# A two-layer retention and attention trunk: first sweep over three token tiles by weight slab, a later turn of the last residual tile, and a tail prepared in the last head

## The chip, the cores and the metric

The kernel runs on one core of one Trainium2 chip. Its engines run side by side: TensorE (PE in the profile, its weight loads PEld), VectorE (DVE), ScalarE (ACT), GpSimd (POOL) and SyncE (SP), which issues DMAs. The metric is the device time of one execution in microseconds (us). Lower is better.

## The reference

Two layers over 1024 tokens of width 1024, all in 32-bit floats. Layer 0 is gated retention with 8 heads (query and key 128 wide, values 256), layer 1 is gated differential attention with 8 heads. Cut to what matters:

```python
h = rmsnorm(x, pre_norm[0]); proj = h @ w_in_a          # q, k, v, gate
o = retention(rope(q), rope(k), v)                      # chunkwise, state carried on, group norm
x = x + rmsnorm((o * silu(gate)) @ w_out_a, post_norm[0])
kv = rmsnorm(x, kv_norm) @ w_kv                         # keys (two per head, rotary), values
h = rmsnorm(x, pre_norm[1]); q, gate = split(h @ w_in_b)
w = softmax(q1 k1) - lam * softmax(q2 k2)               # masked by blocks
o = rmsnorm(w @ v, sub_norm) * (1 - lambda_init)
x = x + rmsnorm((o * silu(gate)) @ w_out_b, post_norm[1])
```

## The kernel before

Tokens are cut into 8 tiles (`c`, `t` or `b`) of 128, the model width into 8 slabs (`s` or `f`) of 128. Every operand of a large product is held as a pair of numbers of a shorter 32-bit form: `split` (L85 on) copies the value into the high part on ACT (L87, or L90 with a gain) and takes the rest into the low part on DVE (L88, L91). `mm3` (L100) multiplies such pairs with three matmuls, high by high, high by low, low by high.

**Retention.** `load_x` brings one tile's transposed x from DRAM and splits it into `xT`; `stats_x` brings the same tile untransposed, sums its squares (L131) and makes scales (L134 to L136) that multiply v and the outputs; `load_qkv` and `load_gate` bring a head's weights. The 64 units (head `h` outside, tile `c` inside) then run in a software pipeline: in unit i, `gemm_qkv` forms q, k and v of tile c in one 512-wide PSUM tile (24 matmuls); `score` of the unit before (L234, mask L235, split L236 and L237) sits in the middle; `rotate` applies the rotary embedding (L207 and L208 on DVE, sum L209 on POOL) and splits v; `combine` of the unit before forms values, carries the state and normalises; `gate_and_transpose` forms the gate (24 matmuls of 256) and transposes q and k (L218, L219), followed on ACT by a copy, Silu (L221) and splits. The first two units share one sweep (`early`): for each slab, tile 0 and then tile 1.

**First output projection.** It runs in two groups of heads. The last step of a tile makes the residual tile `y` (L373). `fin1(t)` gives two functions that transpose half of it each (`quarter`, L284) and split it into `x2T`. Sixteen `gate_unit`s follow, two halves of the gate's columns times 8 tiles. `woven` says which slab of which gate unit is followed by a turn: the turn of tile 6 lies in unit 0 after slabs 2 and 5, and the turn of tile 7 in unit 1 after slabs 3 and 6.

**Attention.** 64 units again; each forms q, k and v of one head and tile (`gemm_piece`, 24 matmuls of 384), rotates (`rotate_b`, L527 and L528 on DVE, L529 on POOL), and in the next unit transposes (`transpose_b`, L538). `attend` yields, two units behind, the pieces for one block of queries: `scores` (L552; fill and maximum L558 and L559, exponent L560, difference of the two softmaxes L565), `turn` (transposes L577) and `values` (L588, copy L591, norm, and a store to the DRAM buffer `og2d`).

**Tail.** `load_wob` brings and splits the second output projection's weights during head 7. `out_prep(t)` loads `og` and the gate `g` of a tile from DRAM, multiplies them (L626), transposes (L632) and splits. `out_gemm(t)` is a generator of 16 steps of three matmuls, with square and sum (L651), product with the post gain (L652), the norm (L653, L105 and L106, the power on POOL) and the residual (L657) after them. What remains of `attend` is interleaved with its steps.

The program is written as one stream; each engine executes its own instructions in the order that the framework's scheduler gave them, so an instruction that waits holds up those behind it on its engine. All DMAs of before are issued by SP, in order. Staging buffers (`st_`) come from one pool of four. PSUM has two slots each of three kinds, g, s2 (1024 wide) and s.

## Time and profile before

| | us |
|---|---|
| median of 3 runs (lowest, highest) | 1515.81 (1514.84, 1515.99) |
| the profiled execution | 1515.86 |
| its span | 1513.9 |
| PE busy | 1480.3 (98%) |
| DVE busy | 784.6 (52%) |
| ACT busy | 629.5 (42%) |
| POOL busy | 268.9 (18%) |

A row of a timeline gives the start, the duration, the engine, the program's line, the operation, output and inputs with their shapes, how often it stands there in a row, and in brackets the idle time of the engine ahead of it with what ended it. `SPq L658` is a DMA issued by SP, `PEq` the sequencer of PE. Time outside the span (1515.86 less 1513.9, about 2 us) is the launch. An engine's busy share says nothing on which wait ends last; that is read stage by stage, below.

### The profile page before, as it was taken

The numbers are of one execution on the slowest core, as the hardware profiler recorded it, in microseconds if no ns is written. First come the engines' busy times: TensorE is split into PE (matmuls) and PEld (weight loads), VectorE is DVE, ScalarE is ACT, GpSimd is POOL, SyncE is SP. The second block draws the span as 40 slices with busy tenths as digits, with TensorE's granted clock in tenths as the row PEclk, the third lists the DMA queues.
The fourth block names the chain that finished last, engine by engine and source line by source line (L and its number), as shares of the span: only waits on it lengthen the run. The fifth ranks groups of instructions, "written<-read, shape, count | busy, mean of one in ns | idle before, by whom it ended". The sixth has DMA issues, their size and how long they took to land.

```text
span 1513.9 us, 23779 instructions
## 1 busy us (share of the span) xinstructions
PE 1480.3 (98%) x8752; PEld 1297.4 (86%) x8752; DVE 784.6 (52%) x1976; ACT 629.5 (42%) x1607; POOL 268.9 (18%) x470
## 2 busy tenths in 40 slices
PE   6999999999999999999999999999999999998998
PEld 5888998888989888888888788988988988987886
DVE  4764645454545544541155502667567567577443
ACT  5542423242423332332244513556556455555421
POOL 0322221222222222200000000222222222222100
PEclk9999999999999999999999999999999999999999
DMA  7430302021111211252345522011011011023352
GB/s 262 158 111 15 95 18 88 22 77 36 59 53 46 63 54 66 70 184 98 140 167 174 174 70 83 30 32 52 22 41 51 12 52 51 11 93 120 113 173 84
DMA packets 70308, 125.63 MB, mean 83 GB/s; under 512 B 7600, under 2 KB 40752, under 8 KB 70192
## 3 DMA queue, kind: packets, MB, share of 16 engines
q1 hardware_dynamic: 70192, 124.11, 25.1%
q8 instruction: 69, 1.13, 0.3%
q14 instruction: 47, 0.39, 0.1%
HBM read 94.72 MB, written 29.36 MB: 82 GB/s over the span
## 4 chain that ended last, share of the span: by engine, by line
PE 85%; DVE 5%; ACT 3%; DMA 3%; issue 3%; POOL 1%; SPq 0%; DVEq 0%; POOLq 0%; ACTq 0%
PE pg L100 57%; PE ps L100 15%; PE ps L552 3%; PE ps L588 3%; PE ps L577 2%; PE ps L284 1%; ACT pr L560 1%; PE ps L234 1%; DVE wbh L91 1%; DMA stw<-in_wa 1%; DMA xr<-in_x 1%; DMA stg<-in_wa 1%; PE ps L538 1%; PE ps L632 1%; DVE m L559 0%
## 5 line engine op out<-in xcount | busy, mean ns | idle before, releaser
L100 PE MATMUL pg<-wq,xT 128*128 128x512 f32 x1536 | 387.0, 402 | 9.9 <-ACT wq L90 7.2
L100 PEld LDWEIGHTS pg<-wq,xT 128*128 128x128 f32 x1536 | 281.2, 190 | 65.9 <-ACT wq L90 7.2
L100 PE MATMUL pg<-wbh,x2T 128*128 128x384 f32 x1536 | 334.4, 353 | 0.0
L100 PEld LDWEIGHTS pg<-wbh,x2T 128*128 128x128 f32 x1536 | 256.3, 189 | 13.0 <-issue 9.2
L106 POOL TENSOR_TENSOR m<-m,mhalf 128x1 f32<-128x1 f32 x152 | 83.8, 551 | 648.2 <-DVE m L105 556.5
L100 PE MATMUL ps<-wg,xT 128*128 128x256 f32 x1536 | 195.4, 283 | 0.4 <-DVE wg L91 0.4
L100 PEld LDWEIGHTS ps<-wg,xT 128*128 128x128 f32 x1536 | 189.3, 192 | 0.8 <-DVE wg L91 0.7
L560 ACT ACTIVATE pr<-ps,m 128x256 f32<-128x256 f32 (+7 forms) x128 | 94.0, 737 | 91.6 <-DVE m L559 91.6
L209 POOL TENSOR_TENSOR a<-a 128x256 f32<-128x256 f32 x64 | 49.0, 766 | 335.8 <-DVE a L208 329.5
L559 DVE TENSOR_REDUCE m<-ps 128x1 f32<-128x256 f32 (+7 forms) x128 | 91.0, 752 | 0.0
L100 PE MATMUL pg<-wbg,x2T 128*128 128x512 f32 x384 | 88.4, 390 | 0.0
L90 ACT ACTIVATE r<-pg,tabA 128x256 fp32r<-128x256 f32 x64 | 30.1, 470 | 136.9 <-DVE a L208 136.5
L100 PEld LDWEIGHTS pg<-wbg,x2T 128*128 128x128 f32 x384 | 71.8, 188 | 14.8
L235 DVE TENSOR_TENSOR a<-ps,tabA 128x128 f32<-128x128 f32 x64 | 18.5, 290 | 115.6 <-PE ps L234 115.4
L100 PEld LDWEIGHTS ps<-r,r 128*128 128x128 f32 x528 | 72.2, 190 | 6.5 <-DVE r L237 0.8
L100 PE MATMUL ps<-r,r 128*128 128x256 f32 x528 | 74.6, 283 | 0.6 <-DVE r L237 0.4
L588 PE MATMUL ps<-v,wT 128*128 128x128 f32 x576 | 74.7, 275 | 0.0
L588 PEld LDWEIGHTS ps<-v,wT 128*128 128x128 f32 x576 | 73.2, 191 | 0.6 <-DVE m L105 0.4
L529 POOL TENSOR_TENSOR tabB<-tabB 128x256 f32<-128x256 f32 x64 | 48.6, 759 | 127.3 <-DVE tabB L528 127.1
L207 DVE TENSOR_TENSOR a<-pg,tabA 128x256 f32<-128x256 f32 x64 | 27.0, 422 | 81.1 <-PE pg L100 81.0
L236 ACT ACTIVATE r<-a 128x128 fp32r<-128x128 f32 x64 | 19.8, 309 | 111.0 <-DVE a L235 110.9
L100 PE MATMUL pg<-wo,oh 128*128 128x512 f32 x192 | 60.9, 398 | 1.1 <-ACT oh L87 1.1
(143 smaller groups left out, 2360.3 us busy)
## 6 DMA issues: line engine op xcount, KB each, us to landing
stw<-in_wa SPq DMA_DIRECT2D x64, 256.0 KB, 3.0
stb<-in_wbh SPq DMA_DIRECT2D x64, 192.0 KB, 2.4
xr<-in_x SPq DMA_DIRECT2D x16, 512.0 KB, 4.2
stg<-in_wa SPq DMA_DIRECT2D x32, 256.0 KB, 3.2
ogd<-a SPq DMA_DIRECT2D x64, 128.0 KB, 1.9
sto<-in_woa SPq DMA_DIRECT2D x16, 512.0 KB, 3.5
og<-ogd SPq DMA_DIRECT2D x16, 512.0 KB, 4.0
y0d<-y SPq DMA_DIRECT2D x8, 512.0 KB, 2.6
```

Of the source, the lines that this page charges most:

```text
L90: nc.scalar.activation(hi, src, AF.Copy, scale=scale)
L100: nc.tensor.matmul(out, l, r, start=(first and i == 0), stop=(last and i == n - 1))
L106: nc.gpsimd.tensor_tensor(out=out, in0=t, in1=mhalf[:, 0:n], op=ALU.pow)
L207: nc.vector.tensor_tensor(out=o4(t1), in0=q4, in1=cb, op=ALU.mult)
L209: nc.gpsimd.tensor_tensor(out=qk, in0=t1, in1=t2, op=ALU.add)
L236: nc.scalar.activation(ss[:, 0, :], sc, AF.Copy)
L529: nc.gpsimd.tensor_tensor(out=r[:, 2], in0=r[:, 0], in1=r[:, 1], op=ALU.add)
L552: nc.tensor.matmul(sc[t][:, c0 : c0 + n], q[rows, ql, qs], k[rows, kl, 0:n], start=(i == 0), stop=(i == 2))
L559: nc.vector.tensor_reduce(out=nm[:, t : t + 1], in_=sc[t][:, :nk], axis=AX.X, op=ALU.max, negate=True)
L560: nc.scalar.activation(pr[t][:, :nk], sc[t][:, :nk], AF.Exp, bias=nm[:, t : t + 1], accum_out=s_[:, t : t + 1])
L577: nc.tensor.transpose(pt[:, k - k0 : k - k0 + P], w[:, k : k + P], ident)
L588: nc.tensor.matmul(po, wT[:, kb * P : (kb + 1) * P], v[:, kb % 4], start=(kb == 0), stop=(kb == b))
```

## The change

It does three things.

**At the start.** A new input `xE` holds the transposed x of the first three tiles by slab. For each of the 8 slabs, one staging buffer takes `xE` of that slab (192 KB, 1536 bytes in a row) and head 0's q, k, v weights of that slab (256 KB), and both are split. The tables (`dvs`, `cosA`, `ssinA`) are fetched after the fifth slab. The first sweep covers three tiles with nine matmuls in each slab; the third tile's PSUM tile is of kind s. Ahead of it stand a Silu on one column of zeros and four 32-bit matmuls on a tile of zeros, whose result nobody reads. The first three units are written in another order: the gate in two pieces with `score` between them, the rotary early for units 0 and 1 and behind `combine` for unit 2, v's split (`scale_v`) behind the statistics, tile 3's x in unit 1, unit 2's transposes in unit 3 after two slabs.

**In the middle.** The turn of tile 7 moves from gate unit 1 (slabs 3 and 6) to gate unit 2 (slabs 2 and 5).

**In the last head and the tail.** `out_prep` becomes `out_fetch` (loads and products, in two halves) and `out_turn` (one half's transposes and split). `out_fetch(0)` is called in unit (7, 5), `out_turn(0, 0)` and `out_turn(0, 1)` in the last unit after slabs 0 and 2, and four steps of the projection stand before the last `transpose_b`. For later tiles `out_turn` is called at steps 7 and 11 of the projection of the tile before. The norm takes its power ahead of the second half's product, the sum of the halves is part of the scaling instruction, and the last tile's result is made and stored in four quarters, issued by SP and ACT in turn.

```diff
--- before.py
+++ after.py
@@ -114,14 +114,13 @@
+    E = 3
...
@@ -160,24 +159,34 @@
     nc.sync.dma_start(gains, a["gains"])
...
+
+    idle, done = kt([P, 512], "idle"), sm(1)
+    nc.vector.memset(idle, 0.0)
+    nc.scalar.activation(done, idle[:, 0:1], AF.Silu)
+    warm = ps("s2")
+    for _ in range(4):
+        nc.tensor.matmul(warm, idle[:, 0:P], idle, start=True, stop=True)
+
     wq, wg = [], []
-    load_qkv(0, 0, wq)
-    load_qkv(0, 1, wq)
-    load_x(1)
-    for s in range(2, NS):
-        load_qkv(0, s, wq)
+    for s in range(NS):
+        st = st_([P, D], "st0")
+        xe, w0 = st[:, 0 : E * P], st[:, 512:1024]
+        nc.sync.dma_start(xe, a["xE"][s])
+        nc.sync.dma_start(w0, a["wa"][0, s, :, 0:512])
+        split(xT[0][0][:, s, 0 : E * P], xT[0][1][:, s, 0 : E * P], xe)
+        w = wt([P, 2, 512], f"wq0{s}")
+        split(w[:, 0, :], w[:, 1, :], w0, g_pre0[:, s : s + 1])
+        wq.append(w)
+        if s == 4:
+            nc.sync.dma_start(dvs, a["dvs"])
+            nc.sync.dma_start(cosA, a["cosA"])
+            nc.sync.dma_start(ssinA, a["ssinA"])
     make_identity(nc, ident)
     nc.vector.memset(mhalf, -0.5)
-    nc.sync.dma_start(dvs, a["dvs"])
-    nc.sync.dma_start(cosA, a["cosA"])
-    nc.sync.dma_start(ssinA, a["ssinA"])
     stats_x(0)
     for s in range(0, NS, 2):
         load_gate(0, s, wg)
     nc.sync.dma_start(mask, a["mask"])
-    load_x(2)
-    stats_x(1)
     w_next = (wq, wg)
 
     def xs(c, s):
@@ -208,12 +217,20 @@
...
+    def scale_v(u):
+
+        c, pq = u["c"], u["pq"]
         split(u["v"][:, 0, :], u["v"][:, 1, :], pq[:, 256:512], avec[:, c, u["h"] : u["h"] + 1])
 
-    def gate_and_transpose(u):
-        c, qk, qkT = u["c"], u["qk"], u["qkT"]
-        pgt = u["pp"][:, 0:256]
-        mm3(pgt, [(*xs(c, s), u["wg"][s][:, 0, :], u["wg"][s][:, 1, :]) for s in range(NS)])
+    def gate(u, s0, s1):
+        c, pgt = u["c"], u["pp"][:, 0:256]
+        for s in range(s0, s1):
+            mm3(pgt, [(*xs(c, s), u["wg"][s][:, 0, :], u["wg"][s][:, 1, :])], s == 0, s == NS - 1)
+        if s1 == NS:
+            u["pgt"] = pgt
+
+    def transpose_qk(u):
+        c, qk, qkT, pgt = u["c"], u["qk"], u["qkT"], u["pgt"]
         pt = ps("s", 256)
...
@@ -380,26 +397,47 @@
...
     prev = None
-    early = [ps("g"), ps("g")]
+    early = [ps("g"), ps("g"), ps("s")]
     gemm_qkv(list(enumerate(early)), w_next[0], range(NS))
     for i in range(H * NC):
         h, c = divmod(i, NC)
         if c == 0:
             wq, wg = w_next
         u = {"h": h, "c": c, "wg": wg, "pp": ps("s2", 1024)}
-        u["pq"] = early[i] if i < 2 else ps("g")
-        if i >= 2:
-            gemm_qkv([(c, u["pq"])], wq, range(0, NS // 2))
-        if prev:
+        if i < E:
+
+            u["pq"] = early[i]
+            if i < 2:
+                rotate(u)
+            gate(u, 0, 3)
+            if prev:
+                score(prev)
+            gate(u, 3, NS)
+            if prev:
+                combine(prev)
+            if i >= 2:
+                rotate(u)
+            if i:
+                stats_x(i)
+            if i == 1:
+                load_x(E)
+            scale_v(u)
+        else:
+            u["pq"] = ps("g")
+            gemm_qkv([(c, u["pq"])], wq, range(0, 2))
+            if i == E:
+                transpose_qk(prev)
+            gemm_qkv([(c, u["pq"])], wq, range(2, NS // 2))
             score(prev)
-        if i >= 2:
             gemm_qkv([(c, u["pq"])], wq, range(NS // 2, NS))
-        rotate(u)
-        if prev:
+            rotate(u)
+            scale_v(u)
             combine(prev)
-        gate_and_transpose(u)
+            gate(u, 0, NS)
+        if i != E - 1:
+            transpose_qk(u)
         prev = u
-        if h == 0 and c + 2 < NC:
+        if h == 0 and 1 <= c < NC - 2:
             if c + 3 < NC:
                 load_x(c + 3)
             stats_x(c + 2)
@@ -503,7 +541,8 @@
     for u in range(2 * NC):
...
-        gate_unit(u // NC, u % NC, dict(zip((2 + u, 5 + u), fin1(NC - 2 + u))) if u < 2 else {})
+        late = {0: NC - 2, 2: NC - 1}
+        gate_unit(u // NC, u % NC, dict(zip((2, 5), fin1(late[u]))) if u in late else {})
...
@@ -617,30 +656,33 @@
     def load_wob(f, hi, lo):
         wob[f] = load_wo(a["wob"], f, gsub, hi, lo)
 
-    def out_prep(t):
+    def out_fetch(t):
...
         og, g = st_([P, D], "og"), st_([P, D], "g")
         nc.sync.dma_start(og, og2d[ts_, :])
         nc.sync.dma_start(g, gd[ts_, :])
-        nc.vector.tensor_tensor(out=og, in0=og, in1=g, op=ALU.mult)
-        oh, ol = (w.rearrange("p (f q) -> p f q", f=NS) for w in wo_pair())
-        for q in range(2):
-            pt = ps("s")
-            for j in range(4):
-                f = q * 4 + j
-                nc.tensor.transpose(pt[:, j * P : (j + 1) * P], og[:, f * P : (f + 1) * P], ident)
-            pv = pt.rearrange("p (j q) -> p j q", j=4)
-            split(oh[:, q * 4 : q * 4 + 4, :], ol[:, q * 4 : q * 4 + 4, :], pv)
-        T[t] = oh, ol
+        for hf in range(2):
+            cs = slice(hf * 512, hf * 512 + 512)
+            nc.vector.tensor_tensor(out=og[:, cs], in0=og[:, cs], in1=g[:, cs], op=ALU.mult)
+        T[t] = og, *(w.rearrange("p (f q) -> p f q", f=NS) for w in wo_pair())
+
+    def out_turn(t, q):
+        og, oh, ol = T[t]
...
     def out_gemm(t):
         ts_ = slice(t * P, (t + 1) * P)
-        oh, ol = T.pop(t)
+        _, oh, ol = T.pop(t)
...
-        sq2, sq, r = sm(2), sm(1), sm(1)
+        sq2, ms, r = sm(2), sm(2), sm(1)
         junk = spare
         for hf in range(2):
             cs = slice(hf * 512, hf * 512 + 512)
@@ -649,19 +691,32 @@
                 mm3(py, [(oh[:, f, :], ol[:, f, :], wob[f][0][:, cs], wob[f][1][:, cs])], f == 0, f == 7)
                 yield
             nc.scalar.activation(junk, py, AF.Square, accum_out=sq2[:, hf : hf + 1])
+            nc.vector.tensor_scalar(
+                out=ms[:, hf : hf + 1],
+                in0=sq2[:, hf : hf + 1],
+                scalar1=1.0 / D,
+                scalar2=ms[:, 0:1] if hf else EPS,
+                op0=ALU.mult,
+                op1=ALU.add,
+            )
+            if hf:
+                nc.gpsimd.tensor_tensor(out=r, in0=ms[:, 1:2], in1=mhalf[:, 0:1], op=ALU.pow)
             nc.vector.tensor_tensor(out=y[:, cs], in0=py, in1=gp1[:, cs], op=ALU.mult)
-        nc.vector.tensor_tensor(out=sq, in0=sq2[:, 0:1], in1=sq2[:, 1:2], op=ALU.add)
-        rsqrt(r, sq, 1.0 / D, EPS)
-        for hf in range(2):
-            cs = slice(hf * 512, hf * 512 + 512)
+        n = 2 if t < NC - 1 else 4
+        for i in range(n):
+            cs = slice(i * D // n, (i + 1) * D // n)
             nc.vector.scalar_tensor_tensor(out=y[:, cs], in0=y[:, cs], scalar=r, in1=xr[:, cs], op0=ALU.mult, op1=ALU.add)
-            nc.sync.dma_start(a["out"][ts_, cs], y[:, cs])
+            (nc.scalar if n == 4 and i % 2 else nc.sync).dma_start(a["out"][ts_, cs], y[:, cs])
 
     def outs():
+
         for t in range(NC):
             if t + 1 < NC:
-                out_prep(t + 1)
-            yield from out_gemm(t)
+                out_fetch(t + 1)
+            for step, _ in enumerate(out_gemm(t)):
+                if t + 1 < NC and step in (7, 11):
+                    out_turn(t + 1, step // 8)
+                yield
 
...
         for s in range(NS):
             gemm_piece(pq, w_cur, c, s)
             ahead(h + 3, c, s)
+            if i == H * NC - 1 and s in (0, 2):
+                out_turn(0, s // 2)
             if s == 4 and prev:
                 transpose_b(*prev)
             if s % 2 == 1 and s // 2 < len(pieces):
@@ -687,12 +744,15 @@
                 load_wob(c + 3, wt([P, D], "wobh"), wt([P, D], "wobl"))
             elif c >= 4:
                 load_wob(c - 4, xw[0][:, c - 4], xw[1][:, c - 4])
-    transpose_b(*prev)
+            if c == 5:
+                out_fetch(0)
     for f in range(6, 8):
         load_wob(f, wt([P, D], "wobh"), wt([P, D], "wobl"))
     spare = xt([P, 512], "spare", F32)
-    out_prep(0)
     og_ = outs()
+    for _ in range(4):
+        next(og_)
+    transpose_b(*prev)
     for step in att:
         for p in step:
             p()
@@ -757,6 +817,7 @@
     return {
+        "xE": xT[:3].transpose(2, 1, 0, 3).reshape(NS, P, 3 * P),
         "wbg": wbg,
```

The scheduler moves more than the diff shows. The first place is DVE at the end of the first sweep. Before, from the last gate weights' splits on (L88 with `stx_178` is the split of tile 2's x, L207 and L208 the first rotary, reading `pg_195`, L134 to L136 the statistics of tile 1):

```order
L91 SCALAR_TENSOR_TENSOR wg_29_164<-stg_171,gains,wg_29_164 128x256 x2
L88 TENSOR_TENSOR xT_1_77<-stx_178,xT_0_76 128x8x128
L207 TENSOR_TENSOR a_40_246<-pg_195,tabA 128x2x2x64
L208 TENSOR_TENSOR a_40_246<-pg_195,tabA 128x2x2x64
L105 TENSOR_SCALAR m_187<-m_185 128x1
L134 TENSOR_SCALAR tabA<-tabA,rstd 128x8
L135 TENSOR_SCALAR tabA<-tabA,rstd 128x8
L91 SCALAR_TENSOR_TENSOR r_41_247<-pg_195,tabA,r_41_247 128x256
L136 TENSOR_TENSOR tabA<-tabA 128x8
```

With the change (L216 and L217 are the rotary's new lines, `pg_202` and `pg_203` the PSUM tiles of tiles 0 and 1, L252 and L254 belong to unit 0's score, `stx_383` is tile 3's x):

```order
L216 TENSOR_TENSOR a_37_278<-pg_202,tabA 128x2x2x64
L91 SCALAR_TENSOR_TENSOR wg_30_186<-stg_187,gains,wg_30_186 128x256 x2
L91 SCALAR_TENSOR_TENSOR wg_30_186<-stg_193,gains,wg_30_186 128x256 x2
L217 TENSOR_TENSOR a_37_278<-pg_202,tabA 128x2x2x64
L216 TENSOR_TENSOR a_42_318<-pg_203,tabA 128x2x2x64
L91 SCALAR_TENSOR_TENSOR r_38_279<-pg_202,tabA,r_38_279 128x256
L217 TENSOR_TENSOR a_42_318<-pg_203,tabA 128x2x2x64
L252 TENSOR_TENSOR a_37_278<-ps_333,tabA 128x128
L88 TENSOR_TENSOR xT_1_77<-stx_383,xT_0_76 128x8x128
L254 TENSOR_TENSOR r_39_280<-a_37_278,r_39_280 128x128
```

The rotary of tiles 0 and 1 now stands among the gate weights' splits, with no split of x ahead of it, and the statistics of tile 1 have moved behind it; tile 3's split stands between the two instructions of unit 0's score.

The second place is PE at the end of the last head, `ps_14573` before and `ps_14651` after being the last pair's transposes (L538, now L577 by the new line numbers). Before:

```order
L552 MATMUL ps_2569_14612<-qk_2495_14301 128x384
L538 MATMUL ps_14573<-ident,tabB 128x128 x2
L632 MATMUL ps_14597<-ident,og_14591 128x128 x4
L100 MATMUL pg_14666<-wob_2497_14307,wo_14596 128x512
L100 MATMUL pg_14666<-wob_2498_14308,wo_14596 128x512
L632 MATMUL ps_14604<-ident,og_14591 128x128 x4
```

With the change (`pg_14638` is the projection of block 0, `wob` and `wo` its weights and its turned input, L591 the last scores):

```order
L100 MATMUL pg_14638<-wob_2498_14326,wo_14417 128x512
L100 MATMUL pg_14638<-wob_2497_14325,wo_14417 128x512 x2
L100 MATMUL pg_14638<-wob_2498_14326,wo_14417 128x512
L100 MATMUL pg_14638<-wob_2497_14325,wo_14417 128x512
L577 MATMUL ps_14651<-ident,tabB 128x128 x2
L591 MATMUL ps_2577_14656<-qk_2417_13971,qk_2495_14319 128x512
L591 MATMUL ps_2578_14657<-qk_2417_13971,qk_2495_14319 128x512
```

The last of twelve matmuls of the output projection now stand ahead of the last transposes, and these ahead of the last scores; the turn of block 0 (L632 before) is no longer behind them.

The third place is DVE in the last two units, from the rotary of unit 61 on (L626 is og times g, L558 and L559 fill and maximum of the scores). Before:

```order
L527 TENSOR_TENSOR tabB<-pg_14313,tabB 128x256
L528 TENSOR_TENSOR tabB<-pg_14313,tabB 128x256
L626 TENSOR_TENSOR og_14591<-og_14591,g_14592 128x1024
L558 MEMSET ps_2519_14400 64x64
L558 MEMSET ps_2520_14401 64x64
L559 TENSOR_REDUCE m_14414<-ps_2519_14400 128x1
L559 TENSOR_REDUCE m_14414<-ps_2520_14401 128x1
```

With the change (L566 and L567 are the rotary, L667 the product, L597 and L598 fill and maximum, L604 the difference of the softmaxes):

```order
L566 TENSOR_TENSOR tabB<-pg_14331,tabB 128x256
L567 TENSOR_TENSOR tabB<-pg_14331,tabB 128x256
L667 TENSOR_TENSOR og_14411<-og_14411,g_14412 128x512 x2
L597 MEMSET ps_2522_14425 64x64
L597 MEMSET ps_2523_14426 64x64
L598 TENSOR_REDUCE m_14439<-ps_2522_14425 128x1
L598 TENSOR_REDUCE m_14439<-ps_2523_14426 128x1
L91 SCALAR_TENSOR_TENSOR wob_2498_14326<-sto_14502,gsub,wob_2497_14325 128x1024
L601 RECIPROCAL m_14449<-m_14440 128x2
```

The product still stands ahead of the fills, now as two instructions, and a split of a wob piece (L91) stands between the maxima and the norm.

More of the change, by code (lines that the diff above doesn't have):

```diff
@@ L115, in yoco_kernel, with load_x @@
     xT = [[xt([P, NS, 512], f"xT{th}{hl}") for hl in range(2)] for th in range(2)]
-    def load_x(c, parts=1):
+    E = 3
+    def load_x(c):
         th, o = c // 4, (c % 4) * P
-        n = NS // parts
         st = st_([P, NS, P], "stx")
-        for i in range(parts):
-            sl = slice(i * n, (i + 1) * n)
-            nc.sync.dma_start(st[:, sl], a["xT"][c, :, sl])
-            split(xT[th][0][:, sl, o : o + P], xT[th][1][:, sl, o : o + P], st[:, sl])
+        nc.sync.dma_start(st, a["xT"][c])
+        split(xT[th][0][:, :, o : o + P], xT[th][1][:, :, o : o + P], st)
     def stats_x(c):
@@ L625, in out_prep @@
         nc.sync.dma_start(g, gd[ts_, :])
-        nc.vector.tensor_tensor(out=og, in0=og, in1=g, op=ALU.mult)
-        oh, ol = (w.rearrange("p (f q) -> p f q", f=NS) for w in wo_pair())
-        for q in range(2):
-            pt = ps("s")
-            for j in range(4):
-                f = q * 4 + j
-                nc.tensor.transpose(pt[:, j * P : (j + 1) * P], og[:, f * P : (f + 1) * P], ident)
-            pv = pt.rearrange("p (j q) -> p j q", j=4)
-            split(oh[:, q * 4 : q * 4 + 4, :], ol[:, q * 4 : q * 4 + 4, :], pv)
-        T[t] = oh, ol
+        for hf in range(2):
[4 more added lines that the diff above has]
+        og, oh, ol = T[t]
+        pt = ps("s")
+        for j in range(4):
+            f = q * 4 + j
+            nc.tensor.transpose(pt[:, j * P : (j + 1) * P], og[:, f * P : (f + 1) * P], ident)
+        pv = pt.rearrange("p (j q) -> p j q", j=4)
+        split(oh[:, q * 4 : q * 4 + 4, :], ol[:, q * 4 : q * 4 + 4, :], pv)
     def out_gemm(t):
         ts_ = slice(t * P, (t + 1) * P)
-        oh, ol = T.pop(t)
+        _, oh, ol = T.pop(t)
         y = kt([P, D], "y")
```

1 line of the change is left out of this document (removed).

## The prediction

> **What bounds the kernel now.** First the page: its first part, then the windows of the start, then the PE timeline with each of its idle rows, and for each the timeline of the engine that ended it.
>
> ```profile
> span 1513.9 us, 23779 instructions
> PE 1480.3 (98%) x8752; PEld 1297.4 (86%) x8752; DVE 784.6 (52%) x1976; ACT 629.5 (42%) x1607; POOL 268.9 (18%) x470
> ```
>
> PE is the bound, and the change removes none of its work. So only time in which PE is idle or runs at half clock can be won. A steady unit of the retention phase shows what PE work costs without stalls (columns: start, duration, work):
>
> ```profile
> 68.21 2.74 PE pg L100 x12
> 70.94 0.22 PE ps L234 x2
> 71.16 2.77 PE pg L100 x12
> 73.94 3.95 PE ps L100 x33
> 77.89 0.11 PE ps L218
> 78.00 0.11 PE ps L219
> 78.11 2.74 PE pg L100 x12
> ```
>
> A 512-wide matmul is 2.74/12 = 0.228 us, a 256-wide one 3.95/33 = 0.12, a transpose (L218, L219) 0.11, a unit 78.11 - 68.21 = 9.90. The windows of the start (length, busy time and count of PE, PEld, DVE, ACT, POOL; then clock, DMA share, GB/s):
>
> ```profile
> 0.00:7.22 7.22, 0.00 (x0) 0.00 (x0) 1.69 (x6) 3.26 (x4) 0.70 (x6) 1.00 0.67 216
> 7.22:12.70 5.48, 5.40 (x11) 3.39 (x12) 3.61 (x5) 3.50 (x5) 0.00 (x0) 1.00 0.85 280
> 12.70:21.23 8.53, 8.53 (x39) 7.02 (x38) 3.79 (x8) 4.80 (x9) 0.56 (x1) 1.00 0.83 263
> ...
> 27.80:33.18 5.38, 0.70 (x5) 0.26 (x3) 2.72 (x8) 3.90 (x7) 1.63 (x3) 1.00 0.93 346
> 33.18:36.60 3.42, 3.38 (x9) 2.83 (x10) 2.04 (x5) 2.73 (x7) 0.55 (x2) 0.50 0.30 92
> ```
>
> Until 12.70 a matmul takes 5.48/11 = 0.50 us, over twice 0.228 (the clock column says 1.00 there only because no clock event stands so early); then 39 run at full pace. Here is what empties PE at 27.80:
>
> ```profile
> 30.21 0.33 PE L218 MATMUL ps<-ident,a 128*128 128x128 f32 x1 [2.15 <-POOL a L209]
> ...
> 33.22 2.05 PE L100 MATMUL pg<-wq,xT 128*128 128x512 f32 x4 [2.57 <-DVE r L91]
> ...
> 27.46 1.23 DVE L88 TENSOR_TENSOR xT<-stx,xT 128x1024 fp32r<-128x1024 f32 x1 [2.79 <-ACT xT L87]
> 28.61 0.42 DVE L207 TENSOR_TENSOR a<-pg,tabA 128x256 f32<-128x256 f32 x1
> ...
> 26.37 1.06 ACT L87 ACTIVATE xT<-stx 128x1024 fp32r<-128x1024 f32 x1 [2.33 <-DMA stx<-in_xT]
> ...
> 30.42 1.28 ACT L221 ACT_TABLE_LOAD   x1
> 31.72 0.47 ACT L221 ACTIVATE a<-ps,rstd 128x256 f32<-128x256 f32 x1
> ```
>
> Tile 2's x lands late, DVE stands at its split, and the first rotary (L207) queues behind it, although the sweep that it reads ended at 21.23; then comes a table load of 1.28.
>
> **The start, worked out.** Up to 68.21 (end of unit 4's transposes) PE's work is five projections (120 x 0.2296 = 27.55, the row pair 2.74 + 2.77), five gates (120 x 0.12 = 14.4), ten transposes (1.1), and for units 0 to 3 score and combine (9.90 less 5.51, 2.87 and 0.22 = 1.30 each, the first unit three matmuls less: 4.8): 47.85 us. It takes 68.21 - 7.22 = 60.99. So 13.1 is lost after the first matmul: 3.0 to slow pace before 12.70 (11 done, room for 24), 2.15 + 2.57 to idle time, 1.7 to half clock from 33.18 on, the rest in small waits.
>
> The change sweeps 72 matmuls (16.4 us) for three tiles, slab by slab. A slab brings 0.20 MB of x and 0.26 MB of weights; at 263 to 280 GB/s 0.459 MB takes 1.64 to 1.75, under the 2.06 of its nine matmuls. With the tables (0.79 MB, after slab 4) 4.46 MB are in by 4.46/0.216 = 20.6 even at the rate of the first window. The last slab then needs its splits (below the first split of the kernel before, the groups of the weight splits):
>
> ```profile
> 4.09 0.63 ACT L87 ACTIVATE xT<-stx 128x512 fp32r<-128x512 f32 x1 [2.07 <-DMA stx<-in_xT]
> ...
> L90 ACT ACTIVATE wq<-stw,gains 128x512 fp32r<-128x512 f32 x9 | 6.5, 724 | 6.0 <-DMA stw<-in_wa 5.9
> L91 DVE SCALAR_TENSOR_TENSOR wq<-stw,gains,wq 128x512 fp32r<-128x512 f32 x9 | 6.7, 751 | 5.6 <-ACT wq L90 5.6
> ```
>
> 0.72 and 0.75 make 1.5: ready by 22.1, when PE is due at it at 21.9. So the sweep is bound by PE. It begins after the new four zero matmuls, 32-bit ones of 512 columns. None stands in the trace; the nearest is the score matmul L234, 32-bit with 128 columns, which is two rows in 0.22. 512 columns are then 4 x 0.22 = 0.88 at full, 1.76 at half clock: 3.5 to 7.0 for four, from about 1.4 on. They end between 4.9 and 8.4, while slab 0 is ready at about 5.8 (the first 0.26 MB of xT had landed at 4.1; now it is 0.46 MB, and the splits). I take 7.5, since half the clock is what the array shows in 7.22:12.70; bounds 6.6 and 8.4. If the zeros open the clock, the sweep ends at 7.5 + 16.4 = 23.9, gate 0 at 26.8. Rotary 0 (two of 0.42 on DVE, 0.77 on POOL) ends near 25.8 under that gate; score 0 lies within gate 1. The Silu table is loaded at the program's start: one load fewer, off the chain. The statistics (L131 and L134 to L136) move behind the rotary and v's split behind them, under gates. What remains: combine 0, due at 30.1, whose rows on ACT and DVE stand behind the split of tile 3's x, landing between 26.5 and 30.4 by the GB/s above (wait 0 to 2.6); combine 1 about 0.7. I take 2.5 lost, 0 to 6 possible (6 is near the 2.33 + 2.79 that the same wait cost ACT and DVE before). Gain: 60.99 + 7.22 - (7.5 + 47.85 + 2.5) = **10.4, I take 10; 6 to 13**.
>
> On the table load: the Trainium skill (ScalarE: Activation LUTs, What ACT_TABLE_LOAD costs) gives 1283 ns and about 1380 ns more for a drain. The load's row agrees (1.28), but the next ACTIVATE starts at 31.72, 0.02 behind it, so no drain is in the trace; with it the sum would be 1.4 lower. On the pieces of 1536 bytes: the skill (DMA: Bandwidth & Descriptors, the table of trn3 B0 against previous generations) wants 2 KiB per partition to saturate the DMAs on previous generations; it would speak against x in slabs and for the first rival.
>
> **The middle.**
>
> ```profile
> 857.57 0.66 PE L284 MATMUL ps<-ident,y 128*128 128x128 f32 x4 [2.35 <-ACT y L373]
> ```
>
> Tile 7's turn waits 2.35 for its y. It now stands 21 matmuls later (21 x 0.228 = 4.8), after other work that was behind it. A delay of 4.8 is more than the wait, so it goes; the x2T that it makes is read only by later gate units of tile 7. Gain **2.4** (1.9 to 2.5).
>
> **The last head.** PE's idle rows, the DVE row behind the first of them, four windows, and the group of the wob splits:
>
> ```profile
> 1384.48 0.66 PE L577 MATMUL ps<-ident,pr 128*128 128x128 f32 x4 [1.62 <-ACT o L591]
> ...
> 1393.11 0.66 PE L577 MATMUL ps<-ident,pr 128*128 128x128 f32 x4 [0.51 <-ACT o L591]
> ...
> 1398.03 0.44 PE L538 MATMUL ps<-ident,tabB 128*128 128x128 f32 x2 [2.04 <-POOL tabB L529]
> ...
> 1399.83 1.22 PE L100 MATMUL pg<-wob,wo 128*128 128x512 f32 x2 [0.69 <-ACT wo L87]
> ...
> 1380.99 1.22 DVE L626 TENSOR_TENSOR og<-og,g 128x1024 f32<-128x1024 f32 x1 [2.35 <-DMA g<-gd]
> ...
> 1382.10:1391.69 9.59, 7.97 (x56) 7.09 (x54) 7.84 (x18) 6.21 (x13) 1.64 (x3) 1.00 0.27 86
> 1391.69:1395.10 3.41, 2.90 (x19) 1.93 (x19) 3.29 (x7) 2.79 (x10) 0.00 (x0) 1.00 0.54 195
> 1395.10:1398.51 3.41, 1.37 (x14) 1.00 (x11) 2.65 (x7) 0.30 (x3) 1.63 (x3) 1.00 0.66 225
> 1398.51:1405.34 6.83, 6.14 (x22) 4.67 (x21) 3.93 (x7) 4.14 (x8) 0.00 (x0) 0.50 0.21 77
> ...
> L91 DVE SCALAR_TENSOR_TENSOR wobl<-sto,gsub,wobh 128x1024 fp32r<-128x1024 f32 x2 | 3.1, 1552 | 0.4 <-ACT wobh L90 0.4
> ```
>
> The idle rows sum to 4.86, and 6.14 of work at half clock loses 3.07: 7.9 in all. DVE stands 2.35 at og times g, ahead of the fills and maxima of the scores; PE's first wait comes from it. The change fetches og and g at c = 5, ahead of two of the wob pieces whose splits take 1.55 each, so block 0's last norm stands earlier by up to 3.1 and DVE's wait should go. But the product itself stays ahead of the fills, and what is late next is DVE. In 1382.10:1398.51 it worked 7.84 + 3.29 + 2.65 = 13.8. The change puts into that stretch two more wob splits (3.1), the two splits of block 0's turn (0.7 each) and half a product (0.6): 18.9. PE worked 7.97 + 2.90 + 1.37 = 12.2 there; the 12 matmuls of the projection (2.74) and the eight transposes of the turn (0.9) make 15.9. So 18.9 - 15.9 = 3.0 of waiting stays, most of it at the last pair's transposes (2.04 now). No stretch is then as empty as 1395.10:1398.51 (1.37 of 3.41), so I let the clock hold. Gain 7.9 - 3.0 = **4.9**; 1 if the clock halves again for such a stretch (3.07 and some waits), 7.9 if DVE hides.
>
> **The end.**
>
> ```profile
> 1507.06 0.60 ACT L651 ACTIVATE spare<-pg 128x512 f32<-128x512 f32 x1 [4.75 <-PE pg L100]
> 1507.78 0.69 DVE L652 TENSOR_TENSOR y<-pg,gp 128x512 f32<-128x512 f32 x1 [4.75 <-ACT spare L651]
> 1508.80 0.55 POOL L106 TENSOR_TENSOR m<-m,mhalf 128x1 f32<-128x1 f32 x1 [10.33 <-DVE m L105]
> 1509.38 1.41 DVE L657 SCALAR_TENSOR_TENSOR y<-y,m,xr 128x512 f32<-128x512 f32 x2 [0.66 <-POOL m L106]
> ```
>
> The power on POOL no longer waits for y's product (0.69) and the sum of the halves: it can begin near 1508.1, so the results start at about 1508.7 instead of 1509.38. Four quarters go on two queues, the last of 128 KB instead of 256, but two more fixed costs per DVE instruction (0.1 each) come in. Gain **0.9** (0.2 to 1.4). The turns of later blocks move into steps 7 and 11 of the projection: PE shows no wait there now, so nothing.
>
> **Sum.** 10 + 2.4 + 4.9 + 0.9 = 18.2. The profiled execution took 1515.86, 0.05 above the median shown (1515.81): 1515.86 - 18.2 = **1497.7**.
>
> **Rivals.** First, transfers bound the start. For: DMA is busy 0.83 to 0.93 in 7.22:33.18, and x comes in pieces of 1536 bytes. Against: 4.46 MB fit even at 216 GB/s. At 180 GB/s the last slab is ready at 4.46/0.18 + 1.5 = 26.3 and the sweep ends at 28.3, 4.4 late: 1502.1. Second, DVE's queue empties PE again before the last scores and the clock halves (the half clock row of 6.83 repeats): the tail gains 1, not 4.9: 1501.6. For it speaks 18.9 against 15.9; against it, that the waits lie apart, with 12 matmuls ahead of the longest. Third, the change does not do what it says: zeros do not open the clock, and as in 7.22:12.70 13 matmuls' room is lost: 13 x 0.228 = 3.0, 1500.7. Fourth, the other side: the array stays at half pace through the whole slab-wise sweep, because each slab's arrival leaves a gap: 7.5 + 72 x 0.498 = 43.4 instead of 23.9, 19.5 lost, 1517.2. It decides from a sweep end of 42.1 on (23.9 + 18.2), which by transfers alone needs under 4.46/38.5 = 116 GB/s. Before, the clock opened after 5.5 us in spite of gaps between slabs, which speaks against it.
>
> **How the numbers follow.** Forecast 0.60, first rival 0.13, second 0.16, third 0.07, fourth 0.04. The range 1491 to 1505 holds the forecast's bounds (the start 6 to 13, the tail 1 to 7.9, not all at one end) and the first three rivals singly, and nearly the first two together (1506); it leaves out the fourth. A difference under 0.2% (3.0 us, 1512.8 to 1518.8) can't be told from none: faster 0.93, same 0.04, slower 0.03.
>
> **What would show it.** Start: the first wq matmul at 6.6 to 8.4 at 0.23 pace, the gates from about 24, unit 4's transposes ending near 58 instead of 68.21. Wrong if the matmuls come in groups of nine with idle time <-DVE wq between them (first rival), or run at 0.50 (third, fourth). Middle: no idle row at L284. Last head: idle rows of the same four kinds below 4 in sum and no window of clock 0.50. End: about 6 from the last square on ACT to the span's end, where now it is 1513.9 - 1507.06 = 6.8.

## The result, and the profile after

| | us |
|---|---|
| the kernel before, median (lowest, highest) | 1515.32 (1514.58, 1515.99) |
| the changed kernel, median (lowest, highest) | 1501.57 (1500.56, 1502.87) |
| ratio, with its 95% interval | 0.9907 (0.9895 to 0.9920) |
| the changed kernel once more, beside later runs | 1500.88, ratio 0.9906 (0.9892 to 0.9921) |

It is faster by 13.75, where 18.2 had been forecast (1497.7). The profiled execution took 1502.49, its span is 1500.7, 13.2 under that of before. Where did 13.2 come from? But for the zeros, both traces hold the same PE work, so the lead of the one over the other can be read at any piece of PE work: its start in the trace before less its start in the trace after.

| up to | lead | gained there | forecast |
|---|---|---|---|
| unit 4's transposes | 5.7 | 5.7 | 10 |
| the last unit of the retention phase | 3.8 | -1.9 | 0 |
| the first transposes of the attention phase | 6.4 | 2.6 | 2.4 |
| the last matmul | 12.4 | 6.0 | 4.9 |
| the span's end | 13.2 | 0.8 | 0.9 |

So in this trace the start gave 3.8 instead of 10 (5.7 up to unit 4, and 1.9 of that lost again), and the rest a little more than forecast. Here is PE in the first 55 us after the change, in the timeline (start, duration, work, and in brackets the idle time ahead with what ended it):

```profile
1.45 6.21 PE L168 MATMUL ps<-idle 128*128 128x512 f32 x8 [1.45 <-DVE idle L164]
7.10 1.96 PE L100 MATMUL pg<-wq,xT 128*128 128x512 f32 x6
...
23.87 3.04 PE L100 MATMUL ps<-wg,xT 128*128 128x256 f32 x24
26.75 0.27 PE L235 MATMUL ps<-ident,a 128*128 128x128 f32 x1
...
32.31 0.50 PE L100 MATMUL ps<-r,r 128*128 128x256 f32 x2 [2.10 <-ACT r L253]
32.65 0.27 PE L235 MATMUL ps<-ident,a 128*128 128x128 f32 x1
33.57 1.01 PE L100 MATMUL ps<-r,r 128*128 128x256 f32 x4 [0.65 <-DVE r L254]
...
51.01 0.51 PE L100 MATMUL ps<-r,r 128*128 128x256 f32 x2 [0.45 <-ACT r L253]
...
52.82 0.33 PE L235 MATMUL ps<-ident,a 128*128 128x128 f32 x1 [0.84 <-POOL a L218]
...
62.10 0.27 PE L235 MATMUL ps<-ident,a 128*128 128x128 f32 x1
```

The sweep runs without a gap and ends at 23.87, as forecast (23.9). Then PE stands at unit 0's combine. What it waits for is on ACT and DVE, and behind that on the queue of SP:

```profile
31.00 1.06 ACT L87 ACTIVATE xT<-stx 128x1024 fp32r<-128x1024 f32 x1 [3.31 <-DMA stx<-in_xT]
31.96 0.29 ACT L253 ACTIVATE r<-a 128x128 fp32r<-128x128 f32 x1
...
32.09 1.23 DVE L88 TENSOR_TENSOR xT<-stx,xT 128x1024 fp32r<-128x1024 f32 x1 [3.29 <-ACT xT L87]
33.23 0.29 DVE L254 TENSOR_TENSOR r<-a,r 128x128 fp32r<-128x128 f32 x1
...
20.42 0.46 SPq L310 DMA_DIRECT2D gp<-in_post  x1
22.15 0.34 SPq L127 DMA_DIRECT2D xr<-in_x  x1
22.95 1.54 SPq L122 DMA_DIRECT2D stx<-in_xT  x2
```

Tile 3's x, issued at 22.95 behind the post gain and tile 1's statistics, is there at 31.0. ACT and DVE stand at its split, and unit 0's score (L253, L254), which needs nothing of it, stands behind. The windows around it (columns as in the windows of before):

```profile
26.88:30.21 3.33, 3.33 (x29) 3.13 (x27) 0.29 (x1) 0.75 (x2) 0.78 (x2) 1.00 0.98 399
30.21:33.85 3.64, 0.89 (x5) 0.66 (x6) 1.76 (x3) 2.31 (x3) 0.00 (x0) 1.00 0.10 41
33.85:37.27 3.42, 3.42 (x13) 2.94 (x13) 2.16 (x7) 1.73 (x4) 0.00 (x0) 0.50 0.74 223
```

After a stretch with 0.89 of PE work in 3.64, PE works 3.42 at a clock of 0.50, which costs 1.7 more. It is the picture of before, with another tile.

In the middle, the turn of tile 7 (the first row below) has no idle time ahead of it any more. In the last head, PE's idle rows are the four behind it:

```profile
855.99 0.60 PE L301 MATMUL ps<-ident,y 128*128 128x128 f32 x4
...
1376.87 0.66 PE L616 MATMUL ps<-ident,pr 128*128 128x128 f32 x4 [0.52 <-ACT o L630]
...
1383.23 1.13 PE L627 MATMUL ps<-v,wT 128*128 128x128 f32 x8 [0.21 <-DVE ps L597]
...
1385.81 0.41 PE L577 MATMUL ps<-ident,tabB 128*128 128x128 f32 x2 [0.37 <-DVE wo L88]
...
1391.28 0.44 PE L577 MATMUL ps<-ident,tabB 128*128 128x128 f32 x2 [0.73 <-POOL tabB L568]
```

They sum to 1.83 where 4.86 stood, and no window there has a clock under 1.00. The end, from ACT's last square to the last store:

```profile
1494.63 0.60 ACT L693 ACTIVATE spare<-pg 128x512 f32<-128x512 f32 x1 [4.75 <-PE pg L100]
...
1495.65 0.55 POOL L703 TENSOR_TENSOR m<-m,mhalf 128x1 f32<-128x1 f32 x1 [10.33 <-DVE m L694]
1496.23 1.67 DVE L708 SCALAR_TENSOR_TENSOR y<-y,m,xr 128x256 f32<-128x256 f32 x4
...
1497.15 1.13 ACTq L709 DMA_DIRECT2D out<-y  x2
```

1500.7 - 1494.63 = 6.1, where it was 6.8.

### The profile page after: what moved, and what is told of

Same layout as the page of the kernel before. It is cut to its first block, busy times and chain, and to the rows that moved or that the text cites. A ratio compares the mean times of both kernels' runs of the same rounds, so it can differ in the third digit from the quotient of the medians.

```text
span 1500.7 us, 23837 instructions
## 1 busy us (share of the span) xinstructions
PE 1480.1 (99%) x8760; PEld 1296.2 (86%) x8760; DVE 786.4 (52%) x1991; ACT 630.2 (42%) x1611; POOL 270.4 (18%) x470
## 4 chain that ended last, share of the span: by engine, by line
PE 84%; DVE 4%; issue 3%; ACT 3%; DMA 2%; POOL 1%; POOLq 0%; DVEq 0%; ACTq 0%; SPq 0%
PE pg L100 57%; PE ps L100 14%; PE ps L591 4%; PE ps L627 3%; PE ps L616 2%; PE ps L301 1%; DMA stg<-in_wa 1%; ACT pr L599 1%; DVE wbh L91 1%; PE ps L251 1%; PE ps L577 1%; DVE m L598 1%; PE ps L235 0%; PE ps L675 0%; PE ps L236 0%
## 5 line engine op out<-in xcount | busy, mean ns | idle before, releaser
L100 PE MATMUL pg<-wq,xT 128*128 128x512 f32 x1512 | 379.6, 400 | 0.0
L100 PEld LDWEIGHTS pg<-wq,xT 128*128 128x128 f32 x1512 | 275.4, 189 | 53.8 <-issue 0.5
L106 POOL TENSOR_TENSOR m<-m,mhalf 128x1 f32<-128x1 f32 x144 | 79.7, 553 | 576.8 <-DVE m L105 500.8
L598 DVE TENSOR_REDUCE m<-ps 128x1 f32<-128x256 f32 (+7 forms) x128 | 91.0, 752 | 0.0
L252 DVE TENSOR_TENSOR a<-ps,tabA 128x128 f32<-128x128 f32 x64 | 18.5, 289 | 115.1 <-PE ps L251 113.1
L216 DVE TENSOR_TENSOR a<-pg,tabA 128x256 f32<-128x256 f32 x63 | 26.6, 422 | 78.3 <-PE pg L100 78.3
L253 ACT ACTIVATE r<-a 128x128 fp32r<-128x128 f32 x64 | 19.8, 309 | 106.5 <-DVE a L252 106.5
```

The lines of the kernel that those rows point to most:

```text
L100: nc.tensor.matmul(out, l, r, start=(first and i == 0), stop=(last and i == n - 1))
L106: nc.gpsimd.tensor_tensor(out=out, in0=t, in1=mhalf[:, 0:n], op=ALU.pow)
L216: nc.vector.tensor_tensor(out=o4(t1), in0=q4, in1=cb, op=ALU.mult)
L253: nc.scalar.activation(ss[:, 0, :], sc, AF.Copy)
L598: nc.vector.tensor_reduce(out=nm[:, t : t + 1], in_=sc[t][:, :nk], axis=AX.X, op=ALU.max, negate=True)
```

## The experiments

The questions were three: whether tile 3's x is the cause of the start's missing gain, what the matmuls on zeros are worth, and which edit carries the last head. Since single executions of one kernel differ by some 2 us, the times are given as ratios to the kernel before, measured beside them, and the places in the traces are read as well. A trace is one execution too: five of the traces below share the changed start, and a table further down shows how far they differ.

**Tile 3's x first.** Its load goes ahead of the first statistics and the gate weights.

```diff
+    load_x(E)
     stats_x(0)
...
-            if i == 1:
-                load_x(E)
```

> Tile 3's x (512 KB) is issued right behind the eight slabs, ahead of the first statistics and the gate weights, instead of behind them and the post gain. Theory A (in the changed kernel PE's idle 2.10 at 32.31 and 0.65 at 33.57 and the half clock after them come from tile 3's x, whose split stands on ACT and DVE between the rows of unit 0's score): those two waits fall under 0.3, no half clock between 27 and 40, unit 4's transposes end near 58 instead of 62.3, time about 1497 (4.4 under the changed kernel). Theory B (the transfers as a whole bind: the same bytes must come anyway): the wait moves to the gate weights at 24 to 27 or to later x tiles, unit 4's transposes end at 61 or later, time within 1.5 of the changed kernel's 1501.6.

Measured: 1499.4, ratio 0.9891 (0.9877 to 0.9906). The first three of PE's idle rows behind the sweep:

```profile
26.23 0.33 PE L236 MATMUL ps<-ident,a 128*128 128x128 f32 x1 [0.61 <-POOL a L219]
...
38.45 0.50 PE L100 MATMUL ps<-r,r 128*128 128x256 f32 x2 [0.28 <-ACT r L254]
...
47.87 0.51 PE L100 MATMUL ps<-r,r 128*128 128x256 f32 x2 [0.56 <-ACT r L254]
```

The two waits are gone, and so is every stretch of half clock up to PE's last matmul. Unit 4's transposes begin at 58.9 instead of 62.1. That is 3.2 earlier, of some 4 expected by theory A, but 0.7 of it is not the edit's: the zeros ended earlier in this execution, and the sweep with them, at 23.14 instead of 23.87. A new wait of 0.61 for the rotary took a part, since the gate weights now come later and DVE has their splits ahead of the first rotary. Theory A holds for the cause of the two waits; theory B would have had the transposes at 61 or later. How much the edit gains is read against more traces, below.

**The post gain late.** Its load moves to head 1.

```diff
-    nc.sync.dma_start(gp0, a["post"][0:1, :].to_broadcast([P, D]))
...
+        if i == 2 * NC:
+            nc.vector.tensor_copy(gp0[:, 0:1], rstd[:, NC - 1 : NC])
+            nc.sync.dma_start(gp0, a["post"][0:1, :].to_broadcast([P, D]))
```

> The load of the first post gain (512 KB, spread from one row over 128 partitions, issued at 20.42 just ahead of tile 1's statistics and tile 3's x) is held back until head 1; a one-column copy on DVE is added to do that. Both x splits, tile 3's and tile 4's, now stand ahead of unit 0's score rows on ACT. Theory A1 (this load ahead in the queue makes tile 3's x late): its split on ACT starts 1.5 to 2 earlier than 31.00, but with tile 4's split (1.06) in front PE's idle 2.10 goes to about 1; time 1499 to 1500.5. Rival (the late landing at 31.0 comes from the loads of x themselves, four of 512 KB in flight at once): the split on ACT still starts after 30.3, PE's idle grows by about 1 for the second split, time 1502 to 1503.

Measured: 1498.85, ratio 0.9891 (0.9877 to 0.9906).

```profile
23.05 1.76 SPq L122 DMA_DIRECT2D stx<-in_xT  x2
...
28.53 1.06 ACT L87 ACTIVATE xT<-stx 128x1024 fp32r<-128x1024 f32 x1 [0.89 <-DMA stx<-in_xT]
29.79 1.06 ACT L87 ACTIVATE xT<-stx 128x1024 fp32r<-128x1024 f32 x1 [0.20 <-DMA stx<-in_xT]
...
31.10 0.50 PE L100 MATMUL ps<-r,r 128*128 128x256 f32 x2 [0.94 <-ACT r L253]
```

Issued at 23.05, as late as in the changed kernel, tile 3's x is there at 28.5 instead of 31.0. PE's idle 2.10 went to 0.94. Against this one trace the 512 KB of post gain ahead of it in the queue would account for 2.5 of its lateness, more than the 1.5 to 2 expected. But in five traces that keep the post gain there (the table below) the split starts between 28.67 and 31.00, at 30.1 on average; so some 1.5 is likely, and it is not shown. The half clock stayed, in another place: from 50.86 to 54.27, behind the waits near 48 and 50.

**Both at once,** the two edits above together.

> Tile 3's x early and the post gain's load late, both at once. Theory (one cause: the late landing of tile 3's x; once it is early the post gain stands in nobody's way): within 1 of the run with tile 3's x early alone (0.9891 of the kernel before, 1499.4 there), PE's waits at unit 0's combine under 0.3. Rival (the post gain's load, slow because of its one row, holds up every load behind it, tile 4's x and the gate weights too): another 1.5 gained, 0.988 of the kernel before.

Measured: 1499.55, ratio 0.9894 (0.9878 to 0.9909); no half clock, unit 4's transposes at 59.7. So nothing is added to the first: once tile 3's x is early, the post gain stands in nobody's way there.

**Without the matmuls on zeros.**

```diff
-    warm = ps("s2")
-    for _ in range(4):
-        nc.tensor.matmul(warm, idle[:, 0:P], idle, start=True, stop=True)
```

> The four matmuls on zeros are left out, the rest of the change stays. Theory A (tile 3's x, landing at 31.0, bounds the first units, so that the sweep has some 2 us of slack): the first matmuls run at 0.50 us until about 11 to 12.7, the sweep ends about 3 later (near 27), PE's idle for unit 0's combine shrinks by as much as the sweep is late, time 1501.6 to 1503. Rival (the sweep binds): unit 4's transposes and the end come 3 later, about 1504.6. If the array were open without them, the sweep would end at 23.9 as now and nothing would change.

Measured: 1500.12, ratio 0.9900 (0.9884 to 0.9917), not slower than the changed kernel. The first matmuls and two windows up to the sweep's end:

```profile
5.31 3.29 PE L100 MATMUL pg<-wq,xT 128*128 128x512 f32 x6 [5.31 <-ACT wq L90]
...
5.31:10.44 5.13, 5.13 (x12) 3.72 (x13) 3.98 (x7) 3.81 (x7) 0.00 (x0) 1.00 0.99 331
10.44:24.28 13.84, 13.84 (x62) 11.45 (x61) 8.47 (x20) 8.70 (x18) 0.56 (x1) 1.00 0.90 287
```

Slab 0 is ready at 5.31, and the zeros had held PE until 7.10. Eleven matmuls at the slow pace take 5.13 where they took 2.95; that 2.2 and the 1.8 of earlier start nearly cancel: the gates begin at 24.28 instead of 23.87. Neither theory had this: the sweep did not end 3 later, so its slack behind tile 3's x was never tested. It is tested here, with the first edit (tile 3's x early) and this one together:

> Tile 3's x early, and the four matmuls on zeros left out. In the run without them alone, the first matmul began at 5.31 instead of 7.10 and the first sweep ended 0.4 later than with them (24.06 against 23.65), since the zeros themselves hold PE until 7.1. Theory (the zeros are worth that 0.4 and no more): within 1 of the run with tile 3's x early, 0.9891 of the kernel before; the sweep ends at 23.3 to 24.1. Rival (the slow pace cost 2.2 in that run and was hidden only by the wait for tile 3's x): 2 to 3 slower than the run with tile 3's x early, 0.9905 to 0.991.

Measured: 1498.87, ratio 0.9890 (0.9875 to 0.9905), as with the zeros (0.9891). In the trace unit 4's transposes are at 60.7, 1.8 behind the run with the zeros, 1.7 of that by a half clock from 50.3 to 53.7 that the other run did not have. The zeros are worth some tenths of a microsecond at the sweep; more is not shown.

**Two matmuls on zeros.** With tile 3's x early, and once with the post gain late too.

```diff
-    for _ in range(4):
+    for _ in range(2):
```

> Tile 3's x early and two matmuls on zeros instead of four, the post gain where it was. The first real matmul at 5.3, the sweep's end near 22.5, unit 4's transposes near 58.5 (3.6 ahead of the changed kernel). Theory: 3 to 3.5 under the changed kernel run beside it. Rival: what the start gains is given back at the head boundaries, where the next head's weights are due (in the trace of tile 3's x early alone 2 of 8.5 went there): under 1.5.

> Tile 3's x early, post gain late, and two matmuls on zeros instead of four. Two take 2.8 at half pace and end near 4.5, before slab 0 is ready at 5.3. If the array stays open over that gap, the first sweep runs from 5.3 at 0.23 and ends near 21.8 to 22.5, some 1 earlier than with four: 0.9875 of the kernel before. If the short run of zeros does not open it, the first 11 matmuls run at 0.5 and the sweep ends at 24: 0.989.

Measured: 1500.41, ratio 0.9901 (0.9886 to 0.9916), and 1500.44, ratio 0.9899 (0.9882 to 0.9915). In both the first real matmul starts at 5.3 and the sweep ends at 22.7. But unit 4's transposes are at 58.8 and 59.3, no earlier than with four (58.9). What the sweep gains is lost again by 50:

```profile
23.41 0.33 PE L236 MATMUL ps<-ident,a 128*128 128x128 f32 x1 [0.33 <-POOL a L219]
...
48.12 0.51 PE L100 MATMUL ps<-r,r 128*128 128x256 f32 x2 [1.04 <-ACT r L254]
...
49.93 0.33 PE L236 MATMUL ps<-ident,a 128*128 128x128 f32 x1 [1.08 <-POOL a L219]
```

The last two are waits of the run with tile 3's x early alone (0.56 and 0.84 there), grown: once the first waits are out, units 3 and 4 wait for DVE, ACT and POOL. In the trace whose rows stand here (post gain where it was), the lead at unit 4 was 9.1 and at the end of the retention phase 6.7. The time gained less than 1.5, as the rival says, but that the rest was given back at the head boundaries is not shown: the run with the old start, below, loses 1.6 over the same stretch, with a lead of 0.6 at unit 4.

**The changed kernel again,** without an edit.

> The changed kernel once more, beside the other runs, for a direct comparison: 0.9907 of the kernel before, in the interval 0.9895 to 0.992.

Measured: 1500.88, ratio 0.9906 (0.9892 to 0.9921). Its lead at unit 4 is 5.7 as before, at the end of the retention phase 5.3 instead of 3.8. Of the 1.9 that the first trace lost there, 1.5 is thus not the same from one execution to the next. Three runs further below change the last head alone, so there are five traces of one and the same start:

| trace | sweep's end | tile 3's split on ACT | PE's wait at unit 0's combine | half clock | unit 4's transposes |
|---|---|---|---|---|---|
| the changed kernel | 23.87 | 31.00 | 2.10 + 0.65 | 33.85 to 37.27 | 62.10 |
| once more | 24.32 | 30.55 | 1.20 + 0.65 | 51.87 to 55.29 | 62.12 |
| last transposes ahead | 23.69 | 30.29 | 1.57 + 0.65 | 33.49 to 36.91 | 61.12 |
| fetch and turn late | 23.52 | 28.67 | 0.1 + 0.65 | 50.24 to 53.66 | 60.24 |
| turn late | 23.39 | 29.82 | 0.99 + 0.65 | 32.91 to 36.33 | 60.72 |

The second part of the wait, 0.65, is the same in all; the first goes with the landing of tile 3's x. One half clock of 3.4 comes in each, in three behind this wait and in two behind the waits of units 3 and 4, near 48 to 51. From the sweep's end to unit 4's transposes these five take 36.7 to 38.2 (37.5 on average), the five with tile 3's x early 35.8 to 36.9 (36.4 on average). So the edit is worth some 1.1 there, not the 3.2 of the first pair of traces.

All five runs with tile 3's x early lie below the changed kernel in ratio (0.9890 to 0.9901 against 0.9906 and 0.9907), but so do the two that leave it late, without the post gain (0.9891) or without the zeros (0.9900), and the intervals overlap: some 1 to 2.5 us are likely, and not established by the times.

**The old start with the rest of the change.** The start's edits are taken back as a whole.

> The start is that of the kernel before, the middle, the last head and the tail are the changed ones. If the parts add up as the PE milestones of the two traces say (middle 2.6, last head and tail 6.0, end 0.8), the time is 9.4 under the kernel before, about 1505.9, and the first 850 us run as before. If the start's gain carried part of the later gains, it is above 1508; if the start in truth hindered them, under 1504.

Measured: 1506.24, ratio 0.9937 (0.9922 to 0.9951), 9.95 under the kernel before, beside it. The parts add up. Lead gained in its trace: 2.6 in the middle, 6.1 in the last head up to the last matmul. Between unit 4 and the last unit of the retention phase, where its code is that of before, it loses 1.6 against the trace of before. So the 1.9 of the first table need not come from the change either.

**The last transposes ahead again.** `transpose_b(*prev)` stands ahead of the projection's first four steps.

```diff
-    for _ in range(4):
-        next(og_)
     transpose_b(*prev)
```

> The changed kernel with the last pair's transposes ahead of the output projection again, so that the 12 matmuls stand behind them; fetch and turn stay in the last head. Theory (the 12 matmuls cover DVE's backlog): PE's wait at the last transposes, 0.73 in the changed kernel, grows by about 2.7 to 3.4, the stretch is empty enough for half clock, and the time is 1504.3 to 1507.5 (2.7 to 6 more). Rival (they only change places; the backlog is covered by the work behind as well): under 1 more, no half clock.

Measured: 1501.07, ratio 0.9910 (0.9887 to 0.9934).

```profile
1389.71 0.44 PE L577 MATMUL ps<-ident,tabB 128*128 128x128 f32 x2 [1.36 <-POOL tabB L568]
```

The wait grew from 0.73 to 1.36, and the clock held. The theory is refuted, and the rival came true: not 2.7 but 0.6 depends on the place of the 12 matmuls, because the scheduler filled the place with the 12 score matmuls of the block before (which had stood behind) and two of the projection.

**Fetch and turn as before, and the turn alone.** In the first, block 0's fetch and turn stand behind the last transposes; in the second only its turn, and `out_fetch(0)` stays at c = 5. In both, the projection's first four steps no longer stand ahead of the last transposes. The edit of the first:

```diff
-            if i == H * NC - 1 and s in (0, 2):
-                out_turn(0, s // 2)
...
-            if c == 5:
-                out_fetch(0)
+    transpose_b(*prev)
...
+    out_fetch(0)
+    out_turn(0, 0)
+    out_turn(0, 1)
     og_ = outs()
-    for _ in range(4):
-        next(og_)
-    transpose_b(*prev)
```

> The changed kernel with the last head of before: fetch and turn of block 0 behind the last pair's transposes, no matmuls of the output projection ahead of these. Theory (the gain of the last head, 6.0 by the PE milestones, is the fetch and turn in the last head; the 12 matmuls ahead are worth 0.6): the waits of before come back at the third last pair (1.6), at the last transposes (2.0) and at the first projection matmul (0.7), with half clock after them; time 1506 to 1508. Rival (the later turns at steps 7 and 11 and the new norm make most of the gain): under 1504.

> As the run before, but with the fetch at c = 5 kept: only the turn of block 0 stands behind the last transposes. Theory F (the early fetch removes DVE's wait for g, which held up the scores, and the turn adds splits to DVE in its fullest stretch, so that it is worth little): the wait at the third last pair is under 0.7, the last transposes wait under 1.5, the first projection matmul waits 0.7; time 1502 to 1503.5. Theory T (the turn is what carries it): waits of 2 or more and half clock at the last transposes; time 1505 or more.

Measured: 1504.35, ratio 0.9926 (0.9911 to 0.9941), and 1503.76, ratio 0.9922 (0.9905 to 0.9938). First the one with both late, PE's idle rows, DVE's product and a window:

```profile
1375.56 0.65 PE L616 MATMUL ps<-ident,pr 128*128 128x128 f32 x4 [1.52 <-ACT o L630]
...
1384.19 0.65 PE L616 MATMUL ps<-ident,pr 128*128 128x128 f32 x4 [0.51 <-ACT o L630]
...
1388.85 0.44 PE L577 MATMUL ps<-ident,tabB 128*128 128x128 f32 x2 [1.84 <-POOL tabB L568]
...
1390.40 0.73 PE L100 MATMUL pg<-wob,wo 128*128 128x512 f32 x2 [0.69 <-ACT wo L87]
...
1372.01 1.29 DVE L667 TENSOR_TENSOR og<-og,g 128x512 f32<-128x512 f32 x2 [2.20 <-DMA g<-gd]
...
1386.00:1390.00 4.00, 1.88 (x18) 1.24 (x14) 3.14 (x8) 0.90 (x3) 1.66 (x3) 1.00 0.57 200
1390.00:1397.00 7.00, 6.60 (x38) 5.67 (x39) 5.51 (x10) 3.85 (x10) 1.34 (x2) 1.00 0.23 77
```

All four waits of before are back, 4.56 in sum against 4.86, as the theory said. But the clock did not halve, though the stretch 1386 to 1390 is nearly as empty as that of before, and so the time stays under the expected 1506, and this trace still gains 3.3 in the last head. Then the one with the early fetch:

```profile
1377.15 0.66 PE L616 MATMUL ps<-ident,pr 128*128 128x128 f32 x4 [0.45 <-ACT o L630]
...
1385.21 0.65 PE L616 MATMUL ps<-ident,pr 128*128 128x128 f32 x4 [0.65 <-ACT o L630]
...
1390.72 0.44 PE L577 MATMUL ps<-ident,tabB 128*128 128x128 f32 x2 [2.30 <-POOL tabB L568]
...
1372.92 1.29 DVE L667 TENSOR_TENSOR og<-og,g 128x512 f32<-128x512 f32 x2 [0.78 <-DMA g<-gd]
...
1391.42:1394.83 3.41, 3.41 (x13) 2.53 (x12) 2.70 (x6) 1.79 (x4) 0.00 (x0) 0.50 0.53 172
```

DVE's wait for g falls from 2.20 to 0.78 by the early fetch, and PE's first wait with it, from 1.52 to 0.45. The wait at the last transposes stays (2.30) and is followed by half clock, and the last head gains 2.6. Theory F was right on the first wait and theory T on the last one, and the time lies between both: fetch and turn are both needed, the first for the scores, the second for the last transposes.

## Why the prediction was right, point by point

**What held.** That PE's work is the bound and only its stalls can be won; the slab-wise sweep bound by PE, from 7.1 (7.5 forecast; 6.4 to 7.6 in the other traces with four matmuls on zeros) to 23.87 (23.9). The window from 7.10 to 23.87 moved 305 GB/s in pieces of 1536 and 2048 bytes, and PE did not wait. The Trainium skill (DMA: Bandwidth & Descriptors, the table of trn3 B0 against previous generations) wants 2 KiB per partition to saturate the DMAs; 305 was enough here, and no run here shows whether larger pieces would have moved more. The middle gave 2.6 (2.4), the end 0.8 (0.9).

**Where it failed: the term of 2.5 for what remains lost in the first units.** It was mis-sized. By its own working the loss up to unit 4's transposes is 62.3 - 7.1 - 47.85 = 7.4, outside even the bound of 6, and 5.8 to 6.9 in the four other traces of this start. The wait for tile 3's x at combine 0 was named with 0 to 2.6 and measured 2.10 + 0.65, in the other four 0.75 to 2.2 in all; with this wait taken out, 4.9 and 5.6 stay lost (tile 3's x early, four matmuls on zeros). Three things were left out. First, a half clock (1.7), which came once in each of the five traces, behind this wait or a later one: the prediction priced the clock at the tail and not here. Second, a load that it didn't count ahead of tile 3's x, the post gain's, likely some 1.5 of the lateness. Third, waits in units 3 and 4 (0.45 and 0.84), which stayed in every run with tile 3's x early; that the work moved behind the rotary (statistics, v's split) comes due there is argued and not tested. The change turned the kernel's first wait, tile 2's x ahead of the first rotary, into the same wait one tile on.

That the time lies inside the range is in part the range's width. The start, with 3.8, stayed under its own bounds of 6 to 13, and the last head made up 1.1 of it. The prediction put nothing between unit 4 and the end of the retention phase, where 1.9 was lost; the cause of that stays open, since the second trace lost 0.4 there and the one with the old start 1.6.

**The times of the first two rivals came true, not their mechanisms.** The first gave 1502.1 by slabs at 180 GB/s. The slabs came in time; a transfer behind them was late. The second gave 1501.6, by a tail that gains 1, and the tail gained 6.0. That these agree with 1501.57 is chance.

**The third rival was priced wrongly.** It took 3.0 for a clock that the zeros do not open. They did open it (the first nine real matmuls run at 0.28 on average, and then at 0.23), but they also hold PE while slab 0 is ready; without them the sweep ends 0.4 later. The prediction compared with the start of before, where the first matmul could not begin ahead of 7.22.

**Last head: 6.0 instead of 4.9.** DVE's backlog was put at 3.0 of remaining waits, and 1.83 remained; 7.9 - 1.83 = 6.1. About half of it, 3.1, is the half clock that did not come, and this part is not certain: with the waits of before back, one trace had it (before) and one not (fetch and turn late); the last section shows how these two differ. The mechanism of the second rival is real: it stands in the trace of the late turn (2.30 and half clock), not in that of the change.
